# Two-layer transformer trunk on one core: a fourth Strassen block in the second MLP product, and one classical block whose low parts a DMA adds up

## The chip, the cores and the metric

One core of a Trainium2 chip (trn2) runs the whole program in one launch. The metric is device time in microseconds (us). The kernel before takes 2185.5 us, the median of 3 runs (2184.15 to 2185.83).

## What is computed

The reference is a decoder trunk of two layers in float32: 256 tokens, width 2048. Layer 0 has a gated convolution mixer beside differential attention, layer 1 a forgetting attention with a cumulative gate. Behind each stands the same MLP, and the change lies in its second product:

```python
def _sqrelu_mlp(h, w1, w2):          # h 256 x 2048, w1 2048 x 8192, w2 8192 x 2048
    return jnp.square(jax.nn.relu(h @ w1)) @ w2
...
        h = _rmsnorm(x, norm2_g[l])
        x = x + _sqrelu_mlp(h, mlp_w1[l], mlp_w2[l])
```

## The kernel before

Every float32 product is made of three matmuls in the format fp32r, which keeps fewer bits: each operand is split into a high part (a copy rounded to fp32r) and a low part (the operand less its high part), and high x high, high x low and low x high are summed in PSUM (`products`, L619). The weights are split as they come: `split_w` (L131) lets ScalarE copy the block `raw` to `wh` (L138) and VectorE subtract to get `wl` (L139). Pool `wspl` has 3 buffers each for `wh` and `wl`, and `wraw` 3 for `raw`.

`mlp` (L685) goes over four groups g of 2048 hidden columns. In each, `hidden` (L591) makes eight blocks of 256 hidden columns with `gemm_t` (L531), and leaves each block in a form that the second product wants. Then `gemm_pair` (L624) runs twice, for the output columns n = 0,1 and n = 2,3 (1024 columns each): 16 second products in all (2 layers, 4 groups, 2 column pairs). One second product goes over the eight blocks of 256 rows of w2; `raw` is such a block, 256 x 1024, as four pieces 128 x 512, and one DMA of 1 MB on SP's queue loads it. `KINDS` (L560) says how block i is multiplied:

- "C", classical: the 2 x 2 pieces give 8 piece products of three matmuls each, 24 matmuls of 512 columns. VectorE makes one `wl` of 2048 columns.
- "S", Strassen's method in Winograd's form: 7 piece products, 21 matmuls. VectorE first makes four sums of pieces in `T` (L637, L639, L640), then two `wl`, `wa` of 1536 columns (from `raw`) and `wb` of 2048 (from `T`).

The sums go to eight PSUM banks: P2, Q3, Q4 and X (pool `accp`, 4 banks, written by all blocks), and P1, Q5, P7 and P6 (pool `tpp`, 4 banks, written by S blocks alone). One block after the last S block (L664) the four `tpp` banks are combined and added to the residual `xr`: ScalarE copies P1 (L666), VectorE adds P6 and P7 and subtracts from Q5 (L667, L668, L669) and adds two halves to `xr` (L674 twice). I call these the combine. `final` (L678) adds the four `accp` banks to `xr` (L680, four times); it is put into the list `late` and runs when the next product or hidden block has been loaded and split. The next second product needs both pools again; the next hidden block needs two `accp` banks. At the end of layer 0, `done(0)` behind the combine lets layer 1's norm start on its transposes, which also use `tpp`.

A framework's scheduler puts the instructions of each engine in one fixed order when the program is built; on the chip each engine works through its own list, and waits where an operand or a buffer isn't ready. PE is TensorE, DVE VectorE, ACT ScalarE, POOL GpSimd, SP the engine that issues the weight loads.

## Time and profile before

| | |
|---|---|
| median of 3 runs | 2185.5 us |
| the profiled execution | 2182.76 us |
| its span, first to last instruction | 2181.0 us |
| mean granted TensorE clock | 1.000 |
| matmuls | 10724 |
| bytes moved by DMA | 412.08 MB |

The span leaves 1.8 us of the profiled execution outside it. A row of the timeline gives the start and the duration of an instruction; neighbours on one engine overlap a little (DVE by 0.08 us, PE by more, as matmuls are pipelined), so the time that one instruction takes from the engine is the distance between two starts, not the duration.

### The profile page before, as it was taken

To read this page: it belongs to the slowest core of one execution; us is meant where nothing else is said; L and a number is where in the kernel's file an instruction comes from. 1 tells how busy PE (TensorE), PEld (TensorE's weight loads), DVE (VectorE), ACT (ScalarE), POOL (GpSimd) and SP (SyncE) were. 2 spreads that over 40 slices of the span, in tenths; PEclk is the share of its full clock that TensorE was granted. 3 is DMA by queue.
4 is the path that set the end of the run, shared out by engine and by line. 5 is a ranking of instruction groups with operands and counts; after the bars stand their busy time and mean duration, and the time that the engine had idled before them with its cause. 6 is when DMAs were issued, how large, how long until landed. Compare 5 with 4: busy or idle time off the path is not lost.

```text
span 2181.0 us, 26007 instructions
## 1 busy us (share of the span) xinstructions
PE 2168.9 (99%) x10724; PEld 1822.0 (84%) x10724; DVE 1546.9 (71%) x1572; ACT 1053.6 (48%) x1099; POOL 18.8 (1%) x17
## 2 busy tenths in 40 slices
PE   8999999999999999999999999999999999999999
PEld 6887888888888888888888888888888888888887
DVE  5576555779768768867856565566787697687687
ACT  6465443545445444445554454445444444444453
POOL 0000000000000000000000000000000000000000
PEclk9999999999999999999999999999999999999999
DMA  7554555555765765665655555555556656656654
GB/s 258 174 173 155 178 189 193 176 172 197 221 186 173 227 191 179 214 189 183 209 168 190 188 182 173 180 174 180 166 205 217 191 174 217 191 187 210 186 193 152
DMA packets 245241, 412.08 MB, mean 189 GB/s; under 512 B 9367, under 2 KB 144770, under 8 KB 245122
## 3 DMA queue, kind: packets, MB, share of 16 engines
q1 hardware_dynamic: 237264, 405.84, 57.6%
q10 hardware_dynamic: 7858, 4.58, 0.7%
q8 instruction: 84, 1.38, 0.2%
q14 instruction: 35, 0.29, 0.0%
HBM read 408.28 MB, written 2.11 MB: 188 GB/s over the span
## 4 chain that ended last, share of the span: by engine, by line
PE 99%; DMA 0%; DVE 0%; ACT 0%; issue 0%; SPq 0%; ACTq 0%; DVEq 0%
PE acc L550 22%; PE acc L554 11%; PE acc L165 11%; PE acc L167 11%; PE acc L166 11%; PE acc L621 8%; PE acc L622 8%; PE acc L620 8%; PE tp L622 2%; PE tp L620 2%; PE tp L621 2%; PE tp L186 1%; PE tp L307 0%; PE tp L319 0%; PE tp L495 0%; DMA ob<-in_hyb_lk_dram 0%
## 5 line engine op out<-in xcount | busy, mean ns | idle before, releaser
L139 DVE TENSOR_TENSOR wl<-raw,wh 128x2048 fp32r<-128x2048 f32 (+2 forms) x388 | 853.6, 2202 | 485.9 <-ACT wh L138 485.3
L138 ACT CAST wh<-raw 128x2048 fp32r<-128x2048 f32 (+2 forms) x388 | 712.8, 1839 | 595.4 <-PE acc L167 219.2
L550 PE MATMUL acc<-act,wh 128*128 128x512 f32 x2048 | 559.6, 395 | 0.0
L165 PE MATMUL acc<-wh,act 128*128 128x512 f32 x1024 | 413.0, 404 | 1.7 <-ACT wh L138 1.7
L166 PE MATMUL acc<-wl,act 128*128 128x512 f32 x1024 | 401.3, 392 | 2.3 <-DVE wl L139 2.3
L167 PE MATMUL acc<-wh,act 128*128 128x512 f32 x1024 | 401.4, 392 | 0.0
L550 PEld LDWEIGHTS acc<-act,wh 128*128 128x128 f32 x2048 | 350.4, 189 | 47.9 <-DVE act L128 0.6
L554 PEld LDWEIGHTS acc<-act,wl 128*128 128x128 f32 x2048 | 314.2, 189 | 43.4
L554 PE MATMUL acc<-act,wl 128*128 128x256 f32 x2048 | 325.8, 281 | 0.0
L621 PE MATMUL acc<-wl,act 128*128 128x512 f32 x656 | 255.9, 390 | 0.0
L622 PE MATMUL acc<-wh,act 128*128 128x512 f32 x656 | 255.4, 389 | 0.0
L620 PE MATMUL acc<-wh,act 128*128 128x512 f32 x656 | 251.4, 389 | 0.0
L167 PEld LDWEIGHTS acc<-wh,act 128*128 128x128 f32 x1024 | 192.7, 188 | 41.9
L166 PEld LDWEIGHTS acc<-wl,act 128*128 128x128 f32 x1024 | 193.3, 189 | 40.9 <-DVE wl L139 3.5
L165 PEld LDWEIGHTS acc<-wh,act 128*128 128x128 f32 x1024 | 192.9, 189 | 40.3 <-ACT wh L138 2.1
L621 PEld LDWEIGHTS acc<-wl,act 128*128 128x128 f32 x656 | 123.1, 188 | 27.4 <-DVE wl L139 1.8
L620 PEld LDWEIGHTS acc<-wh,act 128*128 128x128 f32 x656 | 123.1, 188 | 25.7
L622 PEld LDWEIGHTS acc<-wh,act 128*128 128x128 f32 x656 | 123.1, 188 | 25.4
L138 ACT CAST wh<-qk 128x2048 fp32r<-128x2048 f32 x48 | 91.8, 1913 | 93.7 <-DVE qk L640 69.2
L139 DVE TENSOR_TENSOR wl<-qk,wh 128x2048 fp32r<-128x2048 f32 x48 | 110.0, 2291 | 27.5 <-ACT wh L138 27.5
L611 ACT COPY qk<-acc 128x256 f32<-128x256 f32 x128 | 47.1, 368 | 150.2 <-PE acc L554 150.2
L621 PE MATMUL tp<-wl,act 128*128 128x512 f32 x192 | 74.8, 389 | 0.0
(173 smaller groups left out, 1582.7 us busy)
## 6 DMA issues: line engine op xcount, KB each, us to landing
raw<-in_mlp_w_dram SPq DMA_DIRECT2D x256, 1024.0 KB, 5.6
raw<-in_fox_w_in_dram SPq DMA_DIRECT2D x48, 1024.0 KB, 5.1
raw<-in_hyb_w_in_dram SPq DMA_DIRECT2D x47, 1024.0 KB, 5.1
raw<-in_hyb_w_out_dram SPq DMA_DIRECT2D x16, 1024.0 KB, 5.1
raw<-in_fox_w_out_dram SPq DMA_DIRECT2D x16, 1024.0 KB, 5.0
ob<-fcd ACTq DMA_DIRECT2D x4, 512.0 KB, 4.6
xr<-in_x_dram SPq DMA_DIRECT2D x3, 512.0 KB, 6.8
raw<-in_hyb_w_in_dram SPq DMA_DIRECT2D x2, 512.0 KB, 5.4
```

The source lines that it names most:

```text
L138: nc.scalar.copy(wh[:, s], src[:, s])
L139: nc.vector.tensor_tensor(wl[:, s], src[:, s], wh[:, s].bitcast(F32), ALU.subtract)
L165: nc.tensor.matmul(acc[t], a.hi[:, k, ts], wh[:, k, :], start=st, stop=False)
L166: nc.tensor.matmul(acc[t], a.hi[:, k, ts], wl[:, k, :], start=False, stop=False)
L167: nc.tensor.matmul(acc[t], a.lo[:, k, ts], wh[:, k, :], start=False, stop=sp)
L186: nc.tensor.transpose(ps[:, t * P:(t + 1) * P], xr[n][:, t, j * P:(j + 1) * P], ident)
L550: nc.tensor.matmul(acc[f], wh[:, 4 * h + k, fs], a.both[:, k, :, :].rearrange("p s t -> p (s t)"), start=st, stop=False)
L554: nc.tensor.matmul(acc[f][:, 2 * P:], wl[:, 4 * h + k, fs], a.hi[:, k, :], start=False, stop=sp)
L611: nc.scalar.copy(fj, acc[j][:, 2 * P:])
L620: nc.tensor.matmul(acc, a[0], b[0], start=not started, stop=False)
L621: nc.tensor.matmul(acc, a[0], b[1], start=False, stop=False)
L622: nc.tensor.matmul(acc, a[1], b[0], start=False, stop=last)
```

## The change

Three things change. First, `KINDS` goes from "SCSCSCCC" to "SCSDSCSC": four S blocks, three C, and one D at i = 3. A D block is classical, with 24 matmuls, but its `wl` isn't made by VectorE: ScalarE writes -1 x `raw`, rounded to fp32r, into `wl`, and two accumulating DMAs of 512 KB each, issued by POOL, read the same weights from HBM once more and add them to it; ScalarE makes `wh` by a second pass. Its matmuls go by parts: 8 high x high, 8 low x high, and last the 8 that read `wl`. Its block is loaded one block early, while i = 2 is in work. Second, as the last S block is now i = 6, the combine comes at i = 7, the last block. Third, the gate weights `gw` and `gws` leave the constant pool: `forget_gates` loads them when it starts, which frees space in SBUF; and the scratch for DMA descriptors is larger.

```diff
-    KINDS = "SCSCSCCC"
+    KINDS = "SCSDSCSC"
...
-            elif "C" in KINDS[i + 1:]:
+            elif i < 3:
                 t = actp.tile([P, 4, 2, 2 * P], F32R, name="act")
...
+        def load(i):
+            raw = wraw.tile([P, 4, CW], F32, name="raw")
+            src = w[r0 + 2 * i * P:r0 + 2 * (i + 1) * P, n * CW:(n + 2) * CW].rearrange("(k p) n -> p k n", p=P)
+            nc.sync.dma_start(raw.rearrange("p (k h) n -> p k (h n)", k=2), src)
+            if KINDS[i] != "D":
+                return raw, None
+
+            wl = wspl.tile([P, 4, CW], F32R, name="wl")
+            nc.scalar.activation(wl, raw, AF.Copy, scale=-1.0)
+            for k in range(2):
+                nc.gpsimd.dma_start(
+                    wl.rearrange("p (k h) n -> p k (h n)", k=2)[:, k], src[:, k], accum_op=ALU.add)
+            return raw, wl
+
+        ahead = {}
         for i, (kind, p) in enumerate(zip(KINDS, pairs)):
...
+            raw, wl = ahead.pop(i, None) or load(i)
+            if KINDS[i + 1:i + 2] == "D":
+                ahead[i + 1] = load(i + 1)
...
+            elif kind == "D":
+                wa = wspl.tile([P, 4, CW], F32R, name="wh"), wl
+                nc.scalar.copy(wa[0], raw)
...
+            elif kind == "D":
+                for q in (0, 2, 1):
+                    for k in range(2):
+                        for bank, t, h in (("P2", 0, 1), ("Q3", 0, 0), ("X", 1, 0), ("Q4", 1, 1)):
+                            nc.tensor.matmul(
+                                B[bank], p.part(k, t)[q // 2], wa[q % 2][:, 2 * k + h, :], start=bank not in live, stop=False)
+                            live.add(bank)
```

How the lists of the engines change shows at three places of VectorE's list, all in group g = 0 of layer 0 (the others repeat them). In these rows L637, L639 and L640 of the kernel before are L654, L656 and L657 of the changed one, L667 to L669 are L694 to L696, L674 is L701, L680 is L707, and in the changed kernel L639 is the negation and L641 the accumulating DMA.

**Place 1**, from the first second product (n = 0) to the next (n = 2). Before, from the low split of the last C block (i = 7) to that of the next product's first S block:

```order
L139 TENSOR_TENSOR wl_3943<-raw_3940,wh_3942 128x2048
L669 TENSOR_TENSOR qk_3903<-tp_3719,qk_3903 128x2x512
L637 TENSOR_TENSOR qk_3972<-raw_3970 128x1024
L674 SCALAR_TENSOR_TENSOR xr_87<-qk_3903,r2_3689,xr_87 128x2x512 x2
L639 TENSOR_TENSOR qk_3972<-qk_3972,raw_3970 128x512
L139 TENSOR_TENSOR wl_3977<-raw_3970,wh_3976 128x1536
L640 TENSOR_TENSOR qk_3972<-qk_3972,raw_3970 128x512
L637 TENSOR_TENSOR qk_4049<-raw_4047 128x1024
L639 TENSOR_TENSOR qk_4049<-qk_4049,raw_4047 128x512
L680 SCALAR_TENSOR_TENSOR xr_87<-acc_3714,r2_3689,xr_87 128x512
L139 TENSOR_TENSOR wl_3981<-qk_3972,wh_3980 128x2048
```

In the changed kernel, the rows directly behind the low split of the last C block (i = 7):

```order
L694 TENSOR_TENSOR qk_3971<-tp_3722,qk_3971 128x512
L656 TENSOR_TENSOR qk_3980<-qk_3980,raw_3978 128x512
L695 TENSOR_TENSOR qk_3971<-tp_3721,qk_3971 128x512
L657 TENSOR_TENSOR qk_3980<-qk_3980,raw_3978 128x512
L696 TENSOR_TENSOR qk_3971<-tp_3720,qk_3971 128x2x512
L139 TENSOR_TENSOR wl_3985<-raw_3978,wh_3984 128x1536
L701 SCALAR_TENSOR_TENSOR xr_87<-qk_3971,r2_3690,xr_87 128x2x512 x2
L139 TENSOR_TENSOR wl_3989<-qk_3980,wh_3988 128x2048
L707 SCALAR_TENSOR_TENSOR xr_87<-acc_3715,r2_3690,xr_87 128x512
L707 SCALAR_TENSOR_TENSOR xr_87<-acc_3716,r2_3690,xr_87 128x512
L707 SCALAR_TENSOR_TENSOR xr_87<-acc_3718,r2_3690,xr_87 128x512
L707 SCALAR_TENSOR_TENSOR xr_87<-acc_3717,r2_3690,xr_87 128x512
```

The next row there is `wl_4028`, the low split of the next product's first C block (2048 columns). The combine (L694 to L701) now stands whole behind the last C split and ahead of the next S block's `wb` split; before, L667 and L668 had gone ahead of this stretch, between the splits of the C blocks i = 5, 6 and 7.

**Place 2**, from the second product of n = 2 to the next group's hidden blocks. Before, the rows behind the split `wl_4187` of i = 6; `wl_4217` is the split of i = 7 and `wl_4247` that of the next hidden block, and `final` comes one hidden split (`wl_4291`) later:

```order
L668 TENSOR_TENSOR qk_4177<-tp_3994,qk_4177 128x512
L139 TENSOR_TENSOR wl_4217<-raw_4214,wh_4216 128x2048
L669 TENSOR_TENSOR qk_4177<-tp_3993,qk_4177 128x2x512
L674 SCALAR_TENSOR_TENSOR xr_87<-qk_4177,r2_3689,xr_87 128x2x512 x2
L139 TENSOR_TENSOR wl_4247<-raw_4244,wh_4246 128x2048
```

In the changed kernel, from the split of i = 7 (`wl_4225`); `wl_4262` and `wl_4306` are splits of the next hidden block, and the first hidden matmul writes the PSUM bank that the first L707 frees:

```order
L139 TENSOR_TENSOR wl_4225<-raw_4222,wh_4224 128x2048
L694 TENSOR_TENSOR qk_4252<-tp_4003,qk_4252 128x512
L139 TENSOR_TENSOR wl_4262<-raw_4259,wh_4261 128x2048
L695 TENSOR_TENSOR qk_4252<-tp_4002,qk_4252 128x512
L139 TENSOR_TENSOR wl_4306<-raw_4303,wh_4305 128x2048
L696 TENSOR_TENSOR qk_4252<-tp_4001,qk_4252 128x2x512
L701 SCALAR_TENSOR_TENSOR xr_87<-qk_4252,r2_3690,xr_87 128x2x512 x2
L707 SCALAR_TENSOR_TENSOR xr_87<-acc_3999,r2_3690,xr_87 128x512
```

Between the split of i = 7 and the first evacuation of an `accp` bank there are now the whole combine and two hidden splits.

**Place 3**, the S block i = 2 of the product n = 2. Before (`wl_4020` is the split of the C block i = 1, `wl_4054` and `wl_4058` are `wa` and `wb` of i = 2, `qk_4114` is the `T` of the S block i = 4):

```order
L139 TENSOR_TENSOR wl_4020<-raw_4017,wh_4019 128x2048
L640 TENSOR_TENSOR qk_4049<-qk_4049,raw_4047 128x512
L139 TENSOR_TENSOR wl_4054<-raw_4047,wh_4053 128x1536
L139 TENSOR_TENSOR wl_4058<-qk_4049,wh_4057 128x2048
L637 TENSOR_TENSOR qk_4114<-raw_4112 128x1024
```

In the changed kernel (`wl_4028`; `wl_4068` and `wl_4072`; `qk_4124` is the `T` of i = 4, made from its load `raw_4122`):

```order
L139 TENSOR_TENSOR wl_4028<-raw_4025,wh_4027 128x2048
L654 TENSOR_TENSOR qk_4063<-raw_4055 128x1024
L656 TENSOR_TENSOR qk_4063<-qk_4063,raw_4055 128x512
L139 TENSOR_TENSOR wl_4068<-raw_4055,wh_4067 128x1536
L657 TENSOR_TENSOR qk_4063<-qk_4063,raw_4055 128x512
L654 TENSOR_TENSOR qk_4124<-raw_4122 128x1024
L139 TENSOR_TENSOR wl_4072<-qk_4063,wh_4071 128x2048
```

The first sum of block i = 4 has moved ahead of the `wb` split of block i = 2, so this split now stands behind a load; the load takes the `raw` buffer that the split `wl_4028` frees.

## Rows read from the trace of the kernel before

**Rows 1.** The page, part 1: busy us (share of the span), instructions of each engine.

```profile
PE 2168.9 (99%) x10724; PEld 1822.0 (84%) x10724; DVE 1546.9 (71%) x1572; ACT 1053.6 (48%) x1099; POOL 18.8 (1%) x17
```

**Rows 2.** The page, part 4: the chain that ended last, shares of the span.

```profile
PE 99%; DMA 0%; DVE 0%; ACT 0%; issue 0%; SPq 0%; ACTq 0%; DVEq 0%
```

**Rows 3.** Windows: us; busy PE, PEld, DVE, ACT, POOL; granted clock; DMA share; GB/s.

```profile
486.00:572.00 86.00, 86.00 (x386) 71.31 (x385) 74.89 (x60) 43.31 (x27) 0.00 (x0) 1.00 0.60 202
572.00:658.00 86.00, 86.00 (x494) 75.20 (x493) 57.40 (x57) 37.72 (x36) 0.00 (x0) 1.00 0.61 189
```

**Rows 4.** Timeline of PE (start us, us, engine, line, instruction), an S block into C.

```profile
511.31 0.39 PE L621 MATMUL acc<-wl,act 128*128 128x512 f32 x1
511.53 0.39 PE L622 MATMUL acc<-wh,act 128*128 128x512 f32 x1
511.76 0.39 PE L620 MATMUL acc<-wh,act 128*128 128x512 f32 x1
511.99 0.39 PE L621 MATMUL acc<-wl,act 128*128 128x512 f32 x1
```

**Rows 5.** Timeline of DVE, same columns: combine of n = 0, start of n = 2.

```profile
509.15 2.29 DVE L139 TENSOR_TENSOR wl<-raw,wh 128x2048 fp32r<-128x2048 f32 x1 [3.10 <-ACT wh L138]
511.36 0.69 DVE L667 TENSOR_TENSOR qk<-tp,qk 128x512 f32<-128x512 f32 x1
511.96 2.28 DVE L139 TENSOR_TENSOR wl<-raw,wh 128x2048 fp32r<-128x2048 f32 x1
...
516.96 1.22 DVE L669 TENSOR_TENSOR qk<-tp,qk 128x1024 f32<-128x1024 f32 x1
518.09 1.22 DVE L637 TENSOR_TENSOR qk<-raw 128x1024 f32<-128x1024 f32 x1
519.22 2.47 DVE L674 SCALAR_TENSOR_TENSOR xr<-qk,r,xr 128x1024 f32<-128x1024 f32 x2
521.62 0.68 DVE L639 TENSOR_TENSOR qk<-qk,raw 128x512 f32<-128x512 f32 x1
522.22 1.75 DVE L139 TENSOR_TENSOR wl<-raw,wh 128x1536 fp32r<-128x1536 f32 x1
523.89 0.69 DVE L640 TENSOR_TENSOR qk<-qk,raw 128x512 f32<-128x512 f32 x1
...
526.35 0.74 DVE L680 SCALAR_TENSOR_TENSOR xr<-acc,r,xr 128x512 f32<-128x512 f32 x1
527.01 2.28 DVE L139 TENSOR_TENSOR wl<-qk,wh 128x2048 fp32r<-128x2048 f32 x1
529.21 2.06 DVE L680 SCALAR_TENSOR_TENSOR xr<-acc,r,xr 128x512 f32<-128x512 f32 x3
531.19 2.28 DVE L139 TENSOR_TENSOR wl<-raw,wh 128x2048 fp32r<-128x2048 f32 x1
```

**Rows 6.** The line L630 that loads w2: who waited for it; issue to landing.

```profile
  DVE qk L637: 4.7, 13
DMA to landing us min/median/max: 4.9/5.2/7.5
```

**Rows 7.** Groups by line and shape: busy us, mean ns of one, idle before.

```profile
L138 ACT CAST wh<-raw 128x2048 fp32r<-128x2048 f32 x332 | 634.0, 1910 | 551.3 <-PE acc L167 219.2 <-PE acc L622 170.5 <-issue 82.8
L128 DVE SCALAR_TENSOR_TENSOR act<-tp,g,act 128x256 fp32r<-128x256 f32 x32 | 13.7, 477 | 11.8 <-ACT act L127 11.8
L127 ACT ACTIVATE act<-tp,g 128x256 fp32r<-128x256 f32 x32 | 13.4, 470 | 8.3 <-PE tp L186 8.3
```

**Rows 8.** Timeline of DVE, the last row of the program's VectorE work.

```profile
2175.33 2.79 DVE L680 SCALAR_TENSOR_TENSOR xr<-acc,r,xr 128x512 f32<-128x512 f32 x4 [5.50 <-PE acc L622]
```

**Rows 9.** Timeline of PE, inside the first product of the program.

```profile
11.03 0.63 PE L166 MATMUL acc<-wl,act 128*128 128x512 f32 x1
11.46 0.63 PE L167 MATMUL acc<-wh,act 128*128 128x512 f32 x1
```

More of the change, by code (lines that the diff above doesn't have):

```diff
@@ L229, in trunk_kernel @@
     GP = 16 * 32 + 96
-    gw = const.tile([P, KT, 16], F32, name="gw")
-    gws = const.tile([P, GP], F32R, name="gws")
     def setup():
@@ L246, in setup @@
         nc.scalar.dma_start(bfb, fox_b_f.broadcast_to([P, 16]))
-        nc.scalar.dma_start(gw, fox_w_in[0, :, 3 * D:3 * D + 16].rearrange("(k p) n -> p k n", p=P))
         nc.gpsimd.memset(mask, 0.0)
@@ L414, in forget_gates @@
     def forget_gates(nm):
+        gt = actp.tile([P, 16 * P], F32R, name="act")
+        gws = gt[:, :GP]
+        gw = work.tile([P, 2 * P], F32, name="y").rearrange("p (k n) -> p k n", n=16)
+        nc.scalar.dma_start(gw, fox_w_in[0, :, 3 * D:3 * D + 16].rearrange("(k p) n -> p k n", p=P))
+        yield
         wv = gws[:, :KT * 32].rearrange("p (k n) -> p k n", n=32)
@@ L627, in gemm_pair @@
         live = set()
+        def load(i):
[11 more added lines that the diff above has]
+        ahead = {}
         for i, (kind, p) in enumerate(zip(KINDS, pairs)):
-            raw = wraw.tile([P, 4, CW], F32, name="raw")
-            nc.sync.dma_start(
-                raw.rearrange("p (k h) n -> p k (h n)", k=2),
-                w[r0 + 2 * i * P:r0 + 2 * (i + 1) * P, n * CW:(n + 2) * CW].rearrange("(k p) n -> p k n", p=P))
+            raw, wl = ahead.pop(i, None) or load(i)
+            if KINDS[i + 1:i + 2] == "D":
+                ahead[i + 1] = load(i + 1)
             more = KINDS[i + 1:]
@@ L763 @@
     from concourse.bass_utils import run_bass_kernel_spmd as _run
-    nc = _bacc.Bacc("TRN2", target_bir_lowering=False, num_devices=1, dynamic_dma_scratch_size=1024)
+    nc = _bacc.Bacc("TRN2", target_bir_lowering=False, num_devices=1, dynamic_dma_scratch_size=4096)
     arrays, args = {}, []
```

## The prediction

> **What bounds the kernel now.** I read the page's first part, then the chain, then the windows of one group, then the timelines of PE and DVE around the combine. PE is busy for 99% of the span [rows 1], and the chain of waits is PE for 99% [rows 2]: the time is the number of matmuls by the distance of their starts, 0.227 us for 512 columns [rows 4] (511.31, 511.53, 511.76, 511.99). PE has no holes in the second MLP products, at 486 to 572 us, nor in the hidden blocks behind them, 572 to 658 us [rows 3]. In the first of these windows DVE is busy for 74.89 of 86 us. It keeps up, but its list has little room, so what counts is the order of that list at the places where PE waits for it. [Rows 5] show how it keeps up: the split of the first C block behind the last S block ends at 511.44 (509.15 + 2.29), and PE starts that C block at 511.76 [rows 4], 0.32 us later. The combine (L667 to L674) then sits between the splits of three C blocks, and nobody waits for it, since PE has 16 us of C blocks before it needs a bank of pool `tpp` again.
>
> **Matmuls saved.** Before, a second product has 3 x 21 + 5 x 24 = 183 matmuls; now it has 4 x 21 + 3 x 24 + 24 = 180. 16 products save 48 matmuls x 0.227 = **-10.9 us**. This is the whole gain, since PE is the bound.
>
> **Work on DVE and ACT.** In each product DVE loses two splits (2 x 2.20) and gains an S block (sums 1.13 + 0.60 + 0.60, splits 1.67 + 2.20 [rows 5]): +1.8 us, 3.6 in a window of 86. ACT gains some 3.4 us a product, as one C block's cast goes, an S block's two come, and the D block adds a pass of 1.91 [rows 7]. On average both still fit [rows 3], so I cost the amounts at nothing; the order is another matter. One more S tile per group to fill in the hidden blocks lies under PE as well (DVE 57.40 of 86 there).
>
> **The combine moves from i = 5 to i = 7.** It now has one C block of PE to hide behind, not three. I count from the end of the last C split, with the lead of 0.32 us that [rows 5] and [rows 4] show for a C block behind an S block.
>
> Place 1, from one product to the next, 8 times. DVE's list up to the end of the next product's first C split, by distances of starts [rows 5]: four of 0.60 (2.40), L696 1.13, the `wa` split 1.67, L701 twice 2.40, the `wb` split 2.20, L707 four times 2.64 (0.66 + 1.98), the C split 2.28 to its end: 14.72 us. PE has in that time 24 matmuls of the last C block, 21 of the S block and one of the next C block: 46 x 0.227 = 10.43, and the lead, 10.75 in all. PE waits 4.0 us. **8 x 4.0 = +32.0 us**.
>
> Place 2, from the second product to a hidden block, 6 times (three groups in each layer). DVE: L694 0.60, split 2.20, L695 0.60, split 2.20, L696 1.13, L701 twice 2.40, the first L707 0.74 to its end: 9.87 us. PE has 0.32 + 24 x 0.227 = 5.76. It waits 4.1 us. **6 x 4.1 = +24.6 us**. Before, the evacuation there ran as the banks were done.
>
> End of layer 0, once: the same 4.1, and then the norm's first pair of ACT 0.47 and DVE 0.48 [rows 7] before attention's first matmul, as its transposes need a bank that the combine frees: **+5 us** (3 to 8). End of the program: DVE sat idle for 5.50 us before the last four L680 [rows 8], and the combine there, 0.60 x 2 + 1.13 + 2.40 = 4.7 us with no splits between, fits into it: 0.
>
> **Place 3: a split behind a load.** In every product the `wb` split of i = 2 now stands behind the first sum of i = 4. From the end of the split of i = 1, which frees the buffer: load 5.2 [rows 6], sum 1.17, split 2.29, about 8.66. PE has 23 matmuls of i = 1 and 13 of i = 2 that don't need `wb`'s low part: 36 x 0.227 = 8.17. The wait is some 0.4 us, plus all by which the load is late; call it d. Before, waits of DVE for such a load came to 4.7 us in 13 cases [rows 6], 0.36 each. What is new is that the D block's two accumulating DMAs go out about when this load does, for the negation and that split both follow PE's work on i = 0, on ACT and DVE. The trace shows no accumulating DMA. Lower bound of d: -0.4, the wait is gone. Upper: a load that meets other traffic lands after at most 7.5 us [rows 6], 2.3 above the median; if an accumulate, which also reads its destination, holds the engines twice as long as a load, d is 4.6. I take 1.5, nearer the 2.3 of two plain loads than either end, and less than it because the first half is ahead. **16 x (0.4 + 1.5) = +30.4 us**; ends 0 and 80.
>
> The Trainium skill ("Trainium Kernel Development and Optimization", Key Constraints) says that DMAs from SP, ACT and POOL run on the same 16 engines and interleave. By that rule alone, with equal shares, d would be the 2.3 of [rows 6] and this term 43, the time 2280; by queues that don't touch each other the term would be 6.4, and the time 2243. The trace of before has no second stream in this stage to tell.
>
> **The accumulating DMA's own deadline.** At n = 2 the negation must wait for the `wl` buffer that `wa` of i = 0 leaves, after that block's 12th matmul. From there PE has 9 + 24 + 21 + 16 = 70 matmuls, 15.9 us, until it reads `wl`; less 1.91 for the negation, 14 us. That is nearly twice the longest load of 1 MB, 7.5 us [rows 6], so I cost it at nothing. At n = 0 there is more room. Without this cover each microsecond beyond 14 would cost up to 16 us in all. POOL has nothing else in this stage [rows 3], and nothing is queued behind these DMAs. On SP the loads keep their order. Loading `gw` later, on ACT's queue, hides behind attention's first projection: 0, or one landing, 6 us, if it doesn't.
>
> **Sum.** -10.9 + 32.0 + 24.6 + 5 + 30.4 = +81.1 us against the profiled execution of 2182.76 us (its span of 2181.0 and 1.8 around it): 2263.9. The median of the runs, 2185.5, is 2.7 above that execution, so I forecast **2267 us**. The leads at 15 places may be off by 0.3 us each, some 4 us; with the lower ends of the other terms that is 2231, with the upper ends 2324.
>
> **Rivals.** (1) *The backlog of DVE never reaches PE*, and the time is 2185.5 - 10.9 = **2174.6**, faster. For it: DVE idles 3.10 us before the C split [rows 5], room for most of a combine. It decides at place 1, where DVE's 14.72 us would have to shrink below 10.75. Against it: the combine's first sum reads P6, which the last S block finishes as it ends, and the list is fixed, so that idle time cannot take it. 4%.
>
> (2) *The accumulating DMAs don't get in the loads' way*: d is about 0, the time 2185.5 - 10.9 + 32.0 + 24.6 + 5 + 6.4 = **2243**. For it: the engines are busy for 60% of the window [rows 3]. 15%.
>
> (3) *The accumulating DMA is slow*: d beyond 4.6, or landing beyond its 14 us; **above 2320**; landing after 16 us, with d at 4.6, would make about 2350. For it: it must also read what it adds to, and POOL issues it, which no row shows for this stage. 13%.
>
> (4) *The clock falls in the waits of 4 us.* After its first wait of the program PE ran at 0.43 us a matmul [rows 9], against 0.227 later, the lower and the higher of its two levels, 1.2 and 2.4 GHz. If ten matmuls did so after each of the waits at place 2 and at the end of layer 0, that would be 7 x 10 x 0.2 = 14 us more: **2281**. Against it: the waits are a small part of any stretch. 6%. The Trainium skill ("TensorE: Matmul & The Clock Gate", Why this matters for your kernels) holds that idle gaps between bursts put the clock back to its lower level; by that rule this rival would be the likeliest, while the trace of before has no gap of that length behind its start to show it.
>
> (5) *The change does little of what it says*: both effects small, within 0.2%. 2%.
>
> **How the numbers follow.** My forecast, with d between about 0.3 and 4, has 60%. The range 2231 to 2322 takes in rivals 2 and 4 and leaves out 1, 3 and 5, about 2 in 10. What a measurement of this kernel can tell from no change is 0.2%, 4.4 us. Slower by more: 60 + 15 + 13 + 6 = 94%. Faster by more: 4%. Same: 2%.
>
> **What would show it.** In the changed kernel PE should have 10676 matmuls at 0.227 us, and holes: at place 1 some 3 us before L624 into a `tpp` bank and 1 more up to the next C block's L624, at place 2 some 4 us before the first L552, all put down to DVE; in each product a hole of 1 to 4 us before an L624 in i = 2, with DVE idle before L654 for a load. PE's share would fall to about 96%. I am wrong if PE shows no holes at i = 7, if the holes are put down to POOL's DMAs at L684, or if the sum of holes differs from some 93 us by more than the terms' ends allow.

## The result, and the profile after

The changed kernel takes **2307.16 us** (median of 6 runs, 2298.11 to 2319.24) against 2185.66 us for the kernel before on the same chip (6 runs, 2184.15 to 2186.44): a ratio of **1.0562, 95% interval 1.0545 to 1.0578**, slower by 5.6%. The forecast was 2267 us and slower, in a range of 2231 to 2322; direction and range held, and the time came out 40 us above the forecast. The profiled execution took 2298.11 us, with a span of 2296.2 and a mean granted clock of 0.985; that of the five other executions was 0.981 to 0.983. In the later run `e11_half_gpsimd` one of four executions took 5588 us, and the median and ratio given there are those of the other three.

The first two rows below are the page's part 1 and the first line of its part 4, the answers to [rows 1, 2]:

```profile
PE 2196.9 (96%) x10676; PEld 1830.2 (80%) x10676; DVE 1588.4 (69%) x1644; ACT 1108.2 (48%) x1131; POOL 47.4 (2%) x49
...
PE 79%; DVE 11%; DMA 5%; ACT 2%; issue 2%; SPq 0%; DVEq 0%; ACTq 0%
```

PE's share of the chain that ended last has gone from 99 to 79%; VectorE has 11% of it and DMA 5%. The account of the time, where a hole is a stretch in which PE stands and waits: PE's idle time is the span less its busy time: 99.3 us, 12.1 before, so 87.2 us more. A hole is some 0.16 us longer than the idle time shown for it, as a matmul is shown with 0.39 us and the next one could start 0.227 after it; for some 31 holes that is 5 us, **92 us of new holes** in all. They had been forecast with 92. PE's busy time has risen by 28.0 us although 48 matmuls (10.9 us) are gone; less those 5 us, the other matmuls have become slower by **34 us**. The mean granted clock says the same: 0.985 now, 1.000 before, and 0.015 x 2296 is 34. 92 + 34 - 10.9 = 115, the difference of the two spans (115.2). The 34 had not been in the forecast.

Which instructions waited, from the groups by line (busy us, mean ns of one, idle before and what ended it):

```profile
L624 PE MATMUL tp<-wl,act 128*128 128x512 f32 x256 | 106.9, 418 | 54.8 <-DVE wl L139 54.8
L552 PE MATMUL acc<-act,wh 128*128 128x512 f32 x2048 | 567.7, 399 | 25.1 <-DVE xr L707 25.1
L624 PE MATMUL acc<-wl,act 128*128 128x512 f32 x320 | 127.5, 398 | 1.8 <-DVE wl L139 1.8
L654 DVE TENSOR_TENSOR qk<-raw 128x1024 f32<-128x1024 f32 x64 | 78.1, 1221 | 55.4 <-DMA raw<-in_mlp_w_dram 54.9
```

L552 is place 2: 25.1 us for 6 holes, 4.18 each as shown. L624 into a `tp` bank is place 1 (8 holes of 2.61, 20.9 us) and place 3 (the other 33.9, in 15 holes). L654 shows where place 3 begins: VectorE waited 54.9 us for loads in 22 cases, 4.7 in 13 before [rows 6].

**Place 2** in VectorE's timeline (start, duration), from the last split of the product:

```profile
568.20 2.29 DVE L139 TENSOR_TENSOR wl<-raw,wh 128x2048 fp32r<-128x2048 f32 x1 [3.15 <-ACT wh L138]
570.40 0.68 DVE L694 TENSOR_TENSOR qk<-tp,qk 128x512 f32<-128x512 f32 x1
571.00 2.28 DVE L139 TENSOR_TENSOR wl<-raw,wh 128x2048 fp32r<-128x2048 f32 x1
573.20 0.68 DVE L695 TENSOR_TENSOR qk<-tp,qk 128x512 f32<-128x512 f32 x1
573.80 2.28 DVE L139 TENSOR_TENSOR wl<-raw,wh 128x2048 fp32r<-128x2048 f32 x1
576.00 1.22 DVE L696 TENSOR_TENSOR qk<-tp,qk 128x1024 f32<-128x1024 f32 x1
577.26 2.48 DVE L701 SCALAR_TENSOR_TENSOR xr<-qk,r,xr 128x1024 f32<-128x1024 f32 x2
579.65 2.72 DVE L707 SCALAR_TENSOR_TENSOR xr<-acc,r,xr 128x512 f32<-128x512 f32 x4
```

and in PE's, same columns, an x4 being four matmuls in a row:

```profile
575.98 0.39 PE L625 MATMUL acc<-wh,v 128*128 128x512 f32 x1
580.54 2.05 PE L552 MATMUL acc<-act,wh 128*128 128x512 f32 x4 [4.18 <-DVE xr L707]
582.39 1.05 PE L556 MATMUL acc<-act,wl 128*128 128x256 f32 x4
...
585.80 1.13 PE L552 MATMUL acc<-act,wh 128*128 128x512 f32 x4
586.77 0.64 PE L556 MATMUL acc<-act,wl 128*128 128x256 f32 x4
```

VectorE runs from 568.20 to the first L707 without a pause, and PE stands from 576.21 (575.98 and the usual 0.227) to 580.54: 4.33 us, forecast 4.1. What the forecast lacked follows at once. Four matmuls of 512 columns take 1.85 us behind the hole (580.54 to 582.39) and 0.97 a little later (585.80 to 586.77). The windows of this stretch (us; busy PE, PEld, DVE, ACT, POOL; granted clock; DMA share; GB/s) say why:

```profile
568.00:576.00 8.00, 8.00 (x37) 6.58 (x36) 7.80 (x5) 4.37 (x4) 0.00 (x0) 1.00 0.52 159
576.00:580.00 4.00, 0.37 (x2) 0.00 (x0) 3.96 (x5) 1.90 (x1) 0.00 (x0) 0.88 1.05 346
580.00:586.00 6.00, 5.46 (x17) 4.71 (x18) 4.57 (x5) 0.00 (x0) 0.00 (x0) 0.51 0.28 96
586.00:592.00 6.00, 6.00 (x36) 5.22 (x35) 1.69 (x1) 1.90 (x1) 0.00 (x0) 1.00 0.52 163
```

The granted clock falls in the hole and stays at 0.51, the lower of the two levels (1.2 of 2.4 GHz), for the 6 us behind it. In that window PE issues 17 matmuls, in the next 36. Before the change this stretch ran at 1.00 [rows 3].

**Place 1** is the same with less: VectorE's list from the last C split to the evacuation, and the hole in PE.

```profile
520.94 2.29 DVE L139 TENSOR_TENSOR wl<-raw,wh 128x2048 fp32r<-128x2048 f32 x1 [1.89 <-ACT wh L138]
...
525.55 1.22 DVE L696 TENSOR_TENSOR qk<-tp,qk 128x1024 f32<-128x1024 f32 x1
526.68 1.75 DVE L139 TENSOR_TENSOR wl<-raw,wh 128x1536 fp32r<-128x1536 f32 x1
528.35 2.48 DVE L701 SCALAR_TENSOR_TENSOR xr<-qk,r,xr 128x1024 f32<-128x1024 f32 x2
530.74 2.28 DVE L139 TENSOR_TENSOR wl<-qk,wh 128x2048 fp32r<-128x2048 f32 x1
532.94 2.72 DVE L707 SCALAR_TENSOR_TENSOR xr<-acc,r,xr 128x512 f32<-128x512 f32 x4
535.58 2.28 DVE L139 TENSOR_TENSOR wl<-raw,wh 128x2048 fp32r<-128x2048 f32 x1
```

```profile
523.51 0.84 PE L623 MATMUL acc<-wh,v 128*128 128x512 f32 x3
...
530.09 0.39 PE L623 MATMUL tp<-wh,act 128*128 128x512 f32 x1
533.08 0.49 PE L624 MATMUL tp<-wl,act 128*128 128x512 f32 x1 [2.61 <-DVE wl L139]
...
535.68 0.63 PE L625 MATMUL tp<-wh,act 128*128 128x512 f32 x1
536.11 0.63 PE L624 MATMUL tp<-wl,act 128*128 128x512 f32 x1
```

PE starts the last C block at 523.51, 0.28 us behind the end of its split (523.23); 0.32 had been taken. From there to the end of the next product's C split (537.86) VectorE's list takes 14.63 us; 14.72 had been summed. The hole in front of L624 is 2.76 us (533.08 - 530.09 - 0.227). The second hole, forecast with 1 us at the C split, is missing here: PE reaches it late, as it runs at half speed (0.43 us from 535.68 to 536.11). It is there in the four of the eight cases in which the clock stayed up (at 1097, 1868, 2060 and 2251 us), with 0.43 to 0.47 us as shown.

**Place 3** begins with a load. VectorE's rows at n = 0 and n = 2, and the two DMA lines (the load L634, then the accumulating DMA L641; issue to landing, min/median/max):

```profile
496.95 1.23 DVE L654 TENSOR_TENSOR qk<-raw 128x1024 f32<-128x1024 f32 x1 [2.56 <-DMA raw<-in_mlp_w_dram]
...
544.93 1.23 DVE L654 TENSOR_TENSOR qk<-raw 128x1024 f32<-128x1024 f32 x1 [2.94 <-DMA raw<-in_mlp_w_dram]
...
DMA to landing us min/median/max: 4.9/5.4/12.1
...
DMA to landing us min/median/max: 8.2/11.2/14.4
```

An accumulating DMA of 512 KB takes 11.2 us where a plain load of 1 MB takes 5.4, and the longest of the loads that the profile times takes 12.1, 7.5 before [rows 6].

### The profile page after: what moved, and what is told of

It is laid out like the page before. It is cut to its first block, busy times and chain, and to the rows that moved or that the text cites. A ratio compares the mean times of both kernels' runs of the same rounds, so it can differ in the third digit from the quotient of the medians.

```text
span 2296.2 us, 26136 instructions
## 1 busy us (share of the span) xinstructions
PE 2196.9 (96%) x10676; PEld 1830.2 (80%) x10676; DVE 1588.4 (69%) x1644; ACT 1108.2 (48%) x1131; POOL 47.4 (2%) x49
## 4 chain that ended last, share of the span: by engine, by line
PE 79%; DVE 11%; DMA 5%; ACT 2%; issue 2%; SPq 0%; DVEq 0%; ACTq 0%
PE acc L552 21%; PE acc L556 11%; PE acc L165 10%; PE acc L167 10%; PE acc L166 10%; DVE wl L139 6%; DMA raw<-in_mlp_w_dram 5%; PE acc L684 4%; PE acc L625 2%; PE acc L624 2%; ACT wh L138 2%; PE acc L623 2%; PE tp L624 2%; PE tp L625 1%; DVE xr L701 1%
## 5 line engine op out<-in xcount | busy, mean ns | idle before, releaser
L139 DVE TENSOR_TENSOR wl<-raw,wh 128x2048 fp32r<-128x2048 f32 (+2 forms) x372 | 809.9, 2178 | 475.3 <-ACT wh L138 474.7
L138 ACT CAST wh<-raw 128x2048 fp32r<-128x2048 f32 (+2 forms) x372 | 675.4, 1816 | 569.2 <-PE acc L167 227.6
L552 PE MATMUL acc<-act,wh 128*128 128x512 f32 x2048 | 567.7, 399 | 25.1 <-DVE xr L707 25.1
L165 PE MATMUL acc<-wh,act 128*128 128x512 f32 x1024 | 413.9, 405 | 1.9 <-ACT wh L138 1.9
L552 PEld LDWEIGHTS acc<-act,wh 128*128 128x128 f32 x2048 | 354.9, 191 | 75.4 <-issue 27.4
L166 PE MATMUL acc<-wl,act 128*128 128x512 f32 x1024 | 401.4, 392 | 2.4 <-DVE wl L139 2.4
L167 PE MATMUL acc<-wh,act 128*128 128x512 f32 x1024 | 400.8, 392 | 0.1
L167 PEld LDWEIGHTS acc<-wh,act 128*128 128x128 f32 x1024 | 192.9, 188 | 43.3 <-DVE act L128 1.2
L166 PEld LDWEIGHTS acc<-wl,act 128*128 128x128 f32 x1024 | 193.4, 189 | 40.9 <-DVE wl L139 3.5
L165 PEld LDWEIGHTS acc<-wh,act 128*128 128x128 f32 x1024 | 193.0, 189 | 41.0 <-issue 2.4
L139 DVE TENSOR_TENSOR wl<-qk,wh 128x2048 fp32r<-128x2048 f32 x64 | 146.5, 2289 | 66.6 <-ACT wh L138 66.6
L624 PE MATMUL tp<-wl,act 128*128 128x512 f32 x256 | 106.9, 418 | 54.8 <-DVE wl L139 54.8
L624 PE MATMUL acc<-wl,act 128*128 128x512 f32 x320 | 127.5, 398 | 1.8 <-DVE wl L139 1.8
L623 PE MATMUL acc<-wh,act 128*128 128x512 f32 x320 | 126.9, 397 | 1.1 <-DVE xr L707 1.1
L625 PE MATMUL acc<-wh,act 128*128 128x512 f32 x320 | 126.9, 396 | 0.0
L654 DVE TENSOR_TENSOR qk<-raw 128x1024 f32<-128x1024 f32 x64 | 78.1, 1221 | 55.4 <-DMA raw<-in_mlp_w_dram 54.9
L624 PEld LDWEIGHTS tp<-wl,act 128*128 128x128 f32 x256 | 50.3, 197 | 74.7 <-DVE wl L139 64.9
L625 PE MATMUL tp<-wh,act 128*128 128x512 f32 x256 | 105.1, 411 | 0.0
## 6 DMA issues: line engine op xcount, KB each, us to landing
wl<-in_mlp_w_dram POOLq DMA_DIRECT2D x32, 512.0 KB, 11.2
```

Source lines behind the costliest of these rows:

```text
L138: nc.scalar.copy(wh[:, s], src[:, s])
L139: nc.vector.tensor_tensor(wl[:, s], src[:, s], wh[:, s].bitcast(F32), ALU.subtract)
L165: nc.tensor.matmul(acc[t], a.hi[:, k, ts], wh[:, k, :], start=st, stop=False)
L166: nc.tensor.matmul(acc[t], a.hi[:, k, ts], wl[:, k, :], start=False, stop=False)
L167: nc.tensor.matmul(acc[t], a.lo[:, k, ts], wh[:, k, :], start=False, stop=sp)
L552: nc.tensor.matmul(acc[f], wh[:, 4 * h + k, fs], a.both[:, k, :, :].rearrange("p s t -> p (s t)"), start=st, stop=False)
```

## The experiments

All times are medians against the kernel before on the same chip. Where a run says nothing else, nothing of the computation is left out.

**The order put back.** `e1_order` keeps the four S blocks and the D block, and brings the last S block back to i = 4.

```diff
-    KINDS = "SCSDSCSC"
+    KINDS = "SSDSSCCC"
```

> Only the order of the blocks differs from the changed kernel: KINDS is SSDSSCCC, so the last S block is i = 4 again and the combine comes at i = 5, with three C blocks of PE behind it as before the change; four S, three C and one D stay, with 10676 matmuls. If the place of the combine in VectorE's list makes the holes at places 1 and 2, and the D block's load no longer collides with the load of an S block whose sum stands ahead of another split, the holes go and with them the low clock: 2175 to 2190 us, granted clock 1.00. If the accumulating DMAs are the main cause, whatever the order, some 36 us of holes before L624 and part of the low clock stay: 2220 to 2250 us.

2237.01 us, ratio 1.0233 (1.0217 to 1.0248), in the second range and some 50 us above the first. The holes at places 1 and 2 are gone. The DMAs' holes come to some 39 us, as the second case has it, but not where it puts them: only 17.4 us, behind late loads, stand before L624, and 21.9 us are new, where PE reads the D block's `wl`.

```profile
L684 PE MATMUL acc<-wl,act 128*128 128x512 f32 x128 | 35.8, 412 | 22.0 <-DMA wl<-in_mlp_w_dram 21.9
```

The accumulating DMA is late itself here, at n = 0, where it goes out beside a load: its first half lands after 9.2 to 10.3 us there, and after 5.5 to 7.2 at n = 2.

**No D block, and no accumulating DMA.** `e2_no_d` makes i = 3 an ordinary C block; `e3_no_accumulate` only leaves the two DMAs out.

```diff
-    KINDS = "SCSDSCSC"
+    KINDS = "SCSCSCSC"
```

> The D block becomes a C block (KINDS is SCSCSCSC): no negation and no accumulating DMA, one more split of 2.2 us per product on VectorE; the combine stays at i = 7. If the order is the cause of places 1 and 2, their holes stay at about 2.8 and 4.35 us and those at place 3 shrink to about 0.4: 2185.7 - 10.9 + 28 + 26 + 5 + 6 = 2240 us at full clock, 2255 to 2265 with the low clock that follows the holes. If the accumulating DMAs cause the loss, the time falls to about 2185 us.

2266.35 us, ratio 1.0366 (1.035 to 1.0382), 1 us above the range with the low clock. The holes at places 1 and 2 stand, eight of about 2.57 us and six of about 4.17 as shown; of place 3 two are left, 0.5 and 0.7 us.

```diff
-            for k in range(2):
-                nc.gpsimd.dma_start(
-                    wl.rearrange("p (k h) n -> p k (h n)", k=2)[:, k], src[:, k], accum_op=ALU.add)
```

> The changed kernel without the two accumulating DMAs of each D block: ScalarE's negated high parts stand in for the low parts, so the low parts of the D block are left out of the result. VectorE's list keeps its work. It isolates the traffic: if the loads are late because of these DMAs, the waits of L654 for raw fall from 54.9 us to about 5 and the holes at place 3 from about 36 us to 6, and the time lies 30 us and part of the low clock lower, 2255 to 2270 us. If the loads are late for another reason, such as the early load of the D block itself, the time stays near 2307 us.

2263.13 us, ratio 1.0358 (1.0341 to 1.0376), 44 us less than the changed kernel. The group of L624 and the first wait for a load:

```profile
L624 PE MATMUL tp<-wl,act 128*128 128x512 f32 x256 | 104.8, 409 | 21.7 <-DVE wl L139 21.4
...
497.47 1.22 DVE L651 TENSOR_TENSOR qk<-raw 128x1024 f32<-128x1024 f32 x1 [1.03 <-DMA raw<-in_mlp_w_dram]
```

Of the 21.7 us, 20.9 are place 1. Without the accumulating DMAs place 3 has two holes of 0.3 us, though the order of VectorE's list is the same: all but 0.5 of its 33.9 us hang on the DMAs.

**The holes filled.** `e4_fill` gives PE useless matmuls in the holes of places 1 and 2, 236 of them (results unused).

```diff
         pairs, half = [], None
+        if c0 > 0:
+            fill = tpp.tile([P, CW], F32, name="tp")
+            both = nm.acts[0].both[:, 0].rearrange("p s t -> p (s t)")
+            for j in range(18):
+                nc.tensor.matmul(fill, both[:, :P], both, start=j == 0, stop=j == 17)
         for i, kind in enumerate(KINDS):
             acc = gemm_t(nm.acts, w, c0 + 2 * i * P)
...
+            if i == 0 and n == 2:
+                for _ in range(16):
+                    nc.tensor.matmul(B["P1"], p.part(0)[0], wa[0][:, 0, :], start=True, stop=True)
             if kind == "S":
```

> The changed kernel with useless matmuls put into the holes: 16 ahead of the first matmul of each product of n = 2 (into P1, overwritten by the next), and 18 into an unused bank ahead of the hidden blocks of groups 1 to 3; 8 x 16 + 6 x 18 = 236 matmuls, 53.5 us of PE. They take the place of idle time only, since VectorE's list is what ends there. If the clock falls because of the holes, filling those at places 1 and 2 keeps it up: granted clock above 0.995 and a time of 2268 to 2285 us, lower than the changed kernel's 2307 although PE does more. If the clock doesn't follow these holes, or its fall costs nothing, the time stays at 2307 us or rises by up to 10.

2274.0 us, ratio 1.0405 (1.0377 to 1.0434): 33 us less than the changed kernel, with more matmuls. VectorE's list is no shorter; PE's waits at places 1 and 2 are filled, and no fall of the clock is left behind them. The mean clock is 0.993 in the profiled execution and up to 0.998 in the others, where above 0.995 had been expected: place 3 still has holes, 22.2 us as shown, and the clock falls behind some of them. The clock's cost goes from 34 to 16 us between the two profiled executions, which are 20 us apart; place 3's holes shrink by 12 us, and the useless matmuls take more time than the holes that they fill. The window that had 0.69 in the changed kernel:

```profile
576.00:584.00 8.00, 8.00 (x37) 6.63 (x36) 7.96 (x6) 3.56 (x2) 0.00 (x0) 1.00 0.98 305
```

**Order and DMA apart.** `e5_order_no_accumulate` is e1_order without the DMAs; `e6_combine_late` is the kernel before, with the combine at the last block (the second diff).

```diff
-    KINDS = "SCSDSCSC"
+    KINDS = "SSDSSCCC"
...
-            for k in range(2):
-                nc.gpsimd.dma_start(
-                    wl.rearrange("p (k h) n -> p k (h n)", k=2)[:, k], src[:, k], accum_op=ALU.add)
```

> KINDS = SSDSSCCC (combine at i = 5, D at i = 2) without the two accumulating DMAs of each D block; the low parts of D's weights are then left out of the result. Order theory (with the combine two blocks from the end DVE's list costs PE nothing; what was left of e1_order's loss came from the accumulating DMAs): no holes at L684, none of over 1 us at L624, granted clock 0.998 or more, 2172 to 2182 us, below the kernel before. Rival (the fourth S block itself is too much for DVE and the loads): L624 keeps holes of 1 us and more behind L654, 2195 to 2235 us.

2176.92 us, ratio 0.9966 (0.9953 to 0.9979): faster than the kernel before by 7.7 us, with the low parts of D left out. Part 1 of its page:

```profile
PE 2161.3 (99%) x10676; PEld 1811.2 (83%) x10676; DVE 1585.7 (73%) x1644; ACT 1106.8 (51%) x1131; POOL 18.4 (1%) x17
```

So the fourth S block pays most of its 10.9 us where the order is right, and all that e1_order loses beyond this, 60 us with what it loses in clock, hangs on the accumulating DMAs.

```diff
-            if i == KINDS.rindex("S") + 1:
+            if i == len(KINDS) - 1:
```

> The kernel before with one change: the combine comes at the last block (i = 7) though the last S block is still i = 4; no fourth S block, no D block. Theory (holes at places 1 and 2 come from where the combine stands in DVE's list, and each is followed by half clock): the combine starts with i = 7 as in the changed kernel, so holes of 2 to 3 us at place 1 (8 times) and 4 us at place 2 (6 times), some 45 us, and a clock of 0.985 to 0.993 that adds 15 to 25: 2240 to 2260 us. Rival (the holes need the fourth S block's extra work on DVE): the sums L667 and L668 read finished banks and slip between the splits, holes below 1 us, 2184 to 2200 us.

2190.57 us, ratio 1.0026 (1.0015 to 1.0038): the range of this run's rival held. A late combine alone costs 6 us, and there are no holes at places 1 and 2. The last two C splits of the product and PE's start on the last C block:

```profile
513.78 4.48 DVE L139 TENSOR_TENSOR wl<-raw,wh 128x2048 fp32r<-128x2048 f32 x2
...
524.46 0.39 PE L620 MATMUL acc<-wh,v 128*128 128x512 f32 x1
```

With the last S block at i = 4 VectorE's last C split ends at 518.26 and PE starts that block at 524.46, a lead of 6.2 us; with S at i = 6 the lead was 0.28. Of the rival's two sums L667 slips ahead of these two splits, L668 does not. It is the place of the last S block that counts, not that of the combine's code.

**Where the DMA reads.** `e7_from_sbuf` takes the weights to be added from `raw` and not again from HBM.

```diff
-                    wl.rearrange("p (k h) n -> p k (h n)", k=2)[:, k], src[:, k], accum_op=ALU.add)
+                    wl.rearrange("p (k h) n -> p k (h n)", k=2)[:, k],
+                    raw.rearrange("p (k h) n -> p k (h n)", k=2)[:, k], accum_op=ALU.add)
```

> The changed kernel with one change: the accumulating DMAs read the weights from raw in SBUF and not again from HBM, 16.8 MB less from HBM; bytes written, issue and order stay. If the loads are late because HBM or the loads' own reads are shared with the second read, the landing of the accumulating DMA falls from 11.2 us to about 6, place 3's holes fall below 1 us each, and the time comes near e3_no_accumulate: 2260 to 2275 us. If the accumulation itself (its read and write of the destination) holds the DMA engines, landing stays at 9 to 12 us, place 3 stays, 2295 to 2315 us.

2315.48 us, ratio 1.0595 (1.0579 to 1.0611), at the upper end of the second range, and the landing of the accumulating DMA is what it was:

```profile
DMA to landing us min/median/max: 8.9/11.2/13.5
```

The second read of HBM is not the cause.

**D early.** `e8_early_d`:

```diff
-    KINDS = "SCSDSCSC"
+    KINDS = "SDCSSSCC"
```

> KINDS = SDCSSSCC: D at i = 1, loaded while i = 0 is in work, and the combine at i = 6, one block earlier than in the changed kernel. Theory (a microsecond of hole costs about 1.5 with the clock): place 1 falls below 1 us each, place 2 to 1 to 2 us; D's accumulation has only the 21 matmuls of i = 0 and its own first 16 as cover, 8.4 us against a landing of 11, so holes of some 3 us at L684 come, 16 times: 2225 to 2260 us. If the accumulation lands sooner here, since it is issued before the loads of the S blocks, or DVE's list still hides it: 2180 to 2200 us.

2219.99 us, ratio 1.016 (1.0145 to 1.0175), a little below the first range, and not for its reason: no PE instruction waited for the accumulating DMA, whose first half landed in 5.5 to 5.8 us each time (in the first group the load before it had landed, and the next went out 4 us later). Places 1 and 2 came as expected (none, and 6 of 0.9). New are holes of 1.5 to 3.1 us in eight C blocks, behind a VectorE that waits for loads, and eight of 0.2 to 0.7 us in S blocks.

```profile
L624 PE MATMUL acc<-wl,act 128*128 128x512 f32 x320 | 128.4, 401 | 16.8 <-DVE wl L139 16.8
...
DMA to landing us min/median/max: 5.5/6.7/11.2
```

**Half by DMA, half by VectorE.** `e9_half` is e1_order with this edit; `e12_half_in_changed` is the changed kernel with the same edit.

```diff
-            nc.scalar.activation(wl, raw, AF.Copy, scale=-1.0)
-            for k in range(2):
-                nc.gpsimd.dma_start(
-                    wl.rearrange("p (k h) n -> p k (h n)", k=2)[:, k], src[:, k], accum_op=ALU.add)
+            nc.scalar.activation(wl[:, 2:], raw[:, 2:], AF.Copy, scale=-1.0)
+            nc.gpsimd.dma_start(wl[:, 2:].rearrange("p h n -> p (h n)"), src[:, 1], accum_op=ALU.add)
...
                 nc.scalar.copy(wa[0], raw)
+                nc.vector.tensor_tensor(wl[:, :2], raw[:, :2], wa[0][:, :2].bitcast(F32), ALU.subtract)
```

> KINDS = SSDSSCCC as in e1_order and e5_order_no_accumulate, but only the second half of D's low parts (two of four pieces) comes from one accumulating DMA of 512 KB; VectorE subtracts the first half (1.1 us more a product). Nothing is left out. Theory (the accumulating DMA collides with the loads while it is under way, and half of it lands before PE needs it): landing of 5 to 8 us, no holes at L684, holes at L624 below 1 us, 2174 to 2184 us, a little slower than e5_order_no_accumulate and faster than the kernel before. Rival (any accumulating DMA beside the loads delays them as much): holes behind L654 stay as in e1_order, 2200 to 2235 us.

**2181.80 us, ratio 0.9989 (0.998 to 0.9998)**: below both kernels, by 2.5 us against the one before, which is within the 0.2% of a measurement. There is no hole above 0.25 us behind the start of the program, and the one DMA of a block lands in half the time that the two took:

```profile
PE 2163.7 (99%) x10676; PEld 1812.0 (83%) x10676; DVE 1603.0 (74%) x1660; ACT 1092.7 (50%) x1131; POOL 33.1 (2%) x33
...
DMA to landing us min/median/max: 5.4/5.6/7.2
```

> The changed kernel (KINDS = SCSDSCSC) with the one edit of e9_half: one accumulating DMA of 512 KB a D block, VectorE subtracts the other half. Theory (the accumulating DMA of 1 MB a block is what delays the loads; the rest is where the combine stands): landing of 5 to 8 us, place 3's holes below 1 us, places 1 and 2 unchanged at 2.6 and 4.2: 2255 to 2275 us. If place 3 comes from its place in VectorE's list alone: its holes of 1.6 to 2 us stay, 2290 to 2310 us.

2318.04 us, ratio 1.061 (1.0564 to 1.0657), above both ranges. The theory of the bytes fell: with half of them place 3 costs more in the profiled execution (L624 into `tp` 63.8 us, not 54.8), and no execution was below 2308 us. The first wait, and the DMA's landing:

```profile
501.43 1.23 DVE L652 TENSOR_TENSOR qk<-raw 128x1024 f32<-128x1024 f32 x1 [5.13 <-DMA raw<-in_mlp_w_dram]
...
DMA to landing us min/median/max: 5.9/7.5/10.1
```

The same load, that of i = 4 at n = 0, took from its issue to the L654, or its like, that waited for it 5.4 us alone (e3_no_accumulate, issued 492.05), 6.95 with the accumulating DMA 0.3 us behind it (changed kernel, issued 490.00), and 9.3 with half of that DMA 0.56 us ahead of it (here, issued 492.14). So the bytes don't decide. The order of issue fits all the products of both runs: in the changed kernel the load goes out 0.3 to 0.6 us ahead of the first DMA in 11 of the 16 and takes 6.8 to 7.1 us; in the other five, all at n = 2, the first DMA is 0.2 to 0.5 us ahead and the load takes 7.0 to 10.9, and the two longest holes of place 3, 4.65 and 5.86 us, follow the two slowest of these loads. Here the DMA is 0.2 to 1.3 us ahead in all 16, and the load takes 7.1 to 9.3. The order was not tried by itself, and in e9_half, where the DMA is 1.1 us ahead of a load at n = 0, VectorE waits for none.

**No DMA at all, and GpSimd.** `e10_all_on_vector` has no D block; `e11_half_gpsimd` is e9_half with the half of VectorE given to GpSimd.

```diff
-    KINDS = "SCSDSCSC"
+    KINDS = "SSCSSCCC"
```

> KINDS = SSCSSCCC: the order of e5_order_no_accumulate with no D block; VectorE makes the fourth C block's low parts too, 2.2 us more a product than in e5_order_no_accumulate. Nothing is left out. By the sums, VectorE then has about as much work in a product as PE (some 40.9 us each). If VectorE has room beside the second products (hidden blocks, where it is busy for two thirds of the time): 2175 to 2190 us, and the accumulating DMA was never needed. If its list is the bound in the products, holes of some 1 us a product behind casts and splits and their clock: 2190 to 2215 us.

2198.1 us, ratio 1.0064 (1.005 to 1.0078): the second case. VectorE's list is the bound in the products: each of the eight of n = 2 has holes of some 0.95 and 0.6 us as shown, put down to ScalarE's casts, the first of which waits for VectorE's sum L657. No fall of the clock follows them (1.00 from 530 to 550 us, with two of them).

```diff
-                nc.vector.tensor_tensor(wl[:, :2], raw[:, :2], wa[0][:, :2].bitcast(F32), ALU.subtract)
+                nc.gpsimd.tensor_tensor(wl[:, :2], raw[:, :2], wa[0][:, :2].bitcast(F32), ALU.subtract)
```

> As e9_half (KINDS = SSDSSCCC, one accumulating DMA of 512 KB a D block), but GpSimd and not VectorE subtracts the first half of D's low parts, so that VectorE's list is as short as in e5_order_no_accumulate. Nothing is left out. If GpSimd (idle in this stage) does it beside VectorE without slowing it: no holes, 2174 to 2180 us, the time of e5_order_no_accumulate, and below e9_half. If the two engines get in each other's way or GpSimd's subtraction is late for PE: holes at the matmuls that read wl or behind VectorE's splits, 2183 to 2215 us.

2216.2 us, ratio 1.0137 (1.0117 to 1.0157): the second case again, 1 us above its range. GpSimd's subtraction and VectorE's sum beside it:

```profile
494.11 2.94 POOL L660 TENSOR_TENSOR wl<-raw,wh 128x1024 fp32r<-128x1024 f32 x1 [3.27 <-ACT wh L659]
...
494.71 3.42 DVE L652 TENSOR_TENSOR qk<-raw 128x1024 f32<-128x1024 f32 x1
```

VectorE's sum takes 3.42 us, 1.22 elsewhere, and ends 1.1 us after GpSimd is done; so it goes in all eight products of n = 0. At n = 2 it is GpSimd that needs 6.2 to 7.3 us in seven of eight, beside a VectorE whose instructions follow each other closely and keep their times but for the last. The Trainium skill ("SBUF — State Buffer", Who interferes with whom) says that a VectorE instruction with two SBUF inputs contends with a GpSimd instruction that reads SBUF; these rows agree.

## Why the prediction was right, and where its size was off

**Matmuls saved, -10.9.** Right in number (10676). How much of it can be had shows in e5_order_no_accumulate: 7.7 us in the median. The other 3 show in the second products: the matmuls of L623 to L625 start 228.7 ns apart on average there, and 227.2 before (2495 matmuls, 3.7 us). What holds them isn't traced.

**Place 1, 8 x 4.0 = 32.0.** The mechanism held, VectorE's list to 0.1 us. As a hole it is 8 x 2.76 = 22.1, 7 x 0.33 = 2.3 ahead of the first L623 that needs a bank from L707, and 4 x 0.6 = 2.4 at the C splits, 27 in all; for the rest PE ran at half speed and so needed the splits later.

**Place 2, 6 x 4.1 = 24.6.** 6 x 4.33 = 26.0. Both places need the last S block at i = 6: e1_order and e5_order_no_accumulate have no holes there. The prediction gave the combine's move as the cause; e6_combine_late shows that the move alone does next to nothing. What made the forecast right was its count from a lead of 0.32 us, which it took from a C block behind an S block, and which holds only there.

**End of layer 0, +5.** Two holes, 0.34 and 2.41 us at 1136 and 1139 us, some 3 in all, and 2 us of clock behind them. The end of the program: 0, as put.

**Place 3, 16 x (0.4 + 1.5) = 30.4.** 33.9 us as shown, some 36 as holes, 2.3 each. The sum is near and its split not: without the DMA there is next to no hole (e3_no_accumulate), so the 0.4 was not there and the DMA makes nearly all of it. That the sum came out near is in part luck: the term took the first DMA to be ahead of the load everywhere, which it was in 5 of 16 products, and put 1.5 us on it. The Trainium skill ("Trainium Kernel Development and Optimization", Key Constraints) has the queues interleave on the same engines; by that rule with equal shares the term was 43, by queues that don't touch 6.4. The trace agrees that they touch, with 36; but e12_half_in_changed is no equal sharing, as half the bytes delayed the load by more. How the engines take turns stays open.

**The DMA's own deadline, 0.** Right here, for no PE instruction waited at L684. Its landing, up to 14.4 us, used up the whole cover of 14, and with less cover, in e1_order, it cost 21.9 us of holes.

**The step that failed is the clock,** which the sum took for nothing and rival 4 for 14 us at 6%: ten matmuls at half speed after each wait at place 2 and at the end of layer 0, on the argument that the waits are a small part of any stretch. It cost 34 us: the clock fell to its lower level, for 3 to 7 us each time, behind all six holes of place 2 (13.7 us), four of the eight of place 1 (8.5), four of the fifteen of place 3 (10.2) and at the end of layer 0 (1.7). At rival 4's own places its size was right, 15 us for 14; what it lacked are the holes at places 1 and 3. The forecast's 92 us of holes and -10.9 made 2264 for the profiled execution (2182.76 + 81.1); with 34 of clock they make the 2298 that it took. At the 0.982 or 0.983 of the executions next to the median the clock costs some 40 us, which is most of the rest up to 2307. That this still lies in the range is luck: the range's upper end was there for a slower DMA at place 3, not for the clock. The Trainium skill ("TensorE: Matmul & The Clock Gate", Why this matters for your kernels) holds that idle gaps between bursts put the clock back to its lower level; the windows above agree, at 0.51. The prediction had quoted it, and then trusted a trace without a hole, which could not speak against it.

The runs with the same 10676 matmuls, side by side: PE's idle time (span less busy time), the mean granted clock, and what it cost (1 less the clock, by the span).

| kernel | PE idle, us | clock | lost, us |
|---|---|---|---|
| e5_order_no_accumulate | 13.4 | 1.000 | 0 |
| e9_half | 14.6 | 1.000 | 0 |
| e10_all_on_vector | 25.7 | 0.999 | 2 |
| e11_half_gpsimd | 38.9 | 0.995 | 11 |
| e8_early_d | 40.2 | 0.996 | 9 |
| e1_order | 53.1 | 0.991 | 20 |
| e3_no_accumulate | 65.1 | 0.984 | 36 |
| e2_no_d | 69.5 | 0.986 | 32 |
| changed kernel | 99.3 | 0.985 | 34 |
| e7_from_sbuf | 107.6 | 0.985 | 35 |
| e12_half_in_changed | 109.3 | 0.975 | 58 |

Above the 13 us that the start of the program takes, a microsecond of hole cost 0.3 to 0.7 us of clock in the runs with holes above 1 us. Holes below 1 us as shown cost none in e10_all_on_vector, whose 2 us are a fall behind the start's own hole at 39 us, and none at place 2 of e8_early_d. The price is no constant of the hole: the same 2.61 us at place 1 were followed by the lower clock in eight of eight cases in e3_no_accumulate and in four of eight in the changed kernel, so that without place 3 the clock cost as much as with it. What decides it isn't shown. From the other side, e4_fill shows the cause by filling the holes of places 1 and 2 and leaving VectorE's list as it was.

## What to carry to other kernels

Where TensorE is the bound, price a new hole of some microseconds at about one and a half times its length (1.3 to 1.7 over the runs here): the clock that it costs is paid behind it, and not behind every hole. Before moving late work such as a combine, look for the block that lets the feeding engine get ahead; here it was the place of the last Strassen block. A DMA that accumulates is no free adder: give it a place where no load goes out beside it and cover of more than its landing beside loads (up to 14.4 us here, over two and a half times the 5.4 of a plain load), or cut it in half, as in e9_half; the half alone did not help at the old place (e12_half_in_changed).

## What the runs showed of the hardware that was not expected

- A single accumulating DMA of 512 KB lands in 5.6 us (median of e9_half), about as long as a plain load of 1 MB; two of them beside a load take 8.2 to 14.4, and reading from SBUF makes no difference (e7_from_sbuf).
- Half of these bytes, issued 0.2 to 1.3 us ahead of a load, held that load longer (7.1 to 9.3 us, e12_half_in_changed) than all of them 0.3 to 0.6 us behind it (6.8 to 7.1 us, changed kernel).
- A single hole of 4.33 us between long stretches of dense work brought the granted clock to its lower level for 3 to 7 us behind it, six times of six (0.51 from 580 to 586 us); a hole of 2.76 us did so in four cases of eight, and in eight of eight in e3_no_accumulate.
- A subtraction on GpSimd slows a VectorE sum that starts during it from 1.22 to 3.42 us (e11_half_gpsimd); beside VectorE instructions that follow each other closely GpSimd's own goes from 2.9 to 7.3 us.
